# Encoder block on one core: where the raw weight tiles of the down projection are placed

## The chip, the cores and the metric

The kernel runs on one core of a Trainium2 chip. The metric is the device time of one execution in microseconds (us), the median of several runs; lower is better. A run is also profiled once: the hardware profiler records the start and the length of the engines' instructions and the transfers. The engines are PE (matmuls; PEld is its weight load), DVE (elementwise), ACT (activations and scaled copies), POOL (here a few elementwise operations and the issue of some transfers) and SP (which here only issues transfers).

## The reference, cut to what matters

One encoder layer over 512 tokens of width 2048 in float32: a combined input projection, two attention mixers, an output projection, and a gated feed-forward part. The change touches the last step of this:

```python
h2 = rmsnorm(x, g_ffn[layer])
gate, up = jnp.split(jnp.einsum('bsd,df->bsf', h2, w_gate_up[layer]), 2, axis=-1)
x = x + jnp.einsum('bsf,fd->bsd', jax.nn.silu(gate) * up, w_down[layer])
return rmsnorm(x, g_final)
```

`w_down` is 5632 x 2048, so the down projection multiplies 512 x 5632 by 5632 x 2048.

## The kernel before

**The product in seven.** A matrix product is done by 2 x 2 blocks with seven products instead of four times two (Winograd's form), called m1 to m7 in the code. Each takes one linear form of the activations (kept in the arena, a tile of 112 KB in each partition) and one of the weights. Weights arrive as raw tiles of 128 x 512 float32 (256 KB, 2 KB in each partition). For one pair of row blocks there are four of them, a, b, c and d. Where a form is a sum or a difference, DVE makes it in place (line 801, in `weights`).

**Three matmuls for one.** A float32 operand is split into a high part, which ACT copies (line 761, `split_hi`), and a low part, which DVE subtracts (line 764, `split_lo`). `mm3` (lines 235 to 237) multiplies high by high, high by low and low by high. The pair of parts stands in one of eight tiles called tw, taken in turn.

**Units.** A unit is one form of one pair: the two parts of its weights and six matmuls of 128 x 512. Units run in the order of a list. `ColBlock` makes the list of a column block: all pairs of m1, then m7 and m6, two units of m2, all of m5, the rest of m2, then m4 and m3. In the code's plan KEPT each raw tile is loaded once for a block and kept: a is last used by m5, b and d by m4, c by m3. When a form is done, ACT evicts two banks (line 1139, tile ev) and POOL adds them to memory by an accumulating transfer (line 1140); unit and bank orders make a few matmuls wait for that eviction.

**The down blocks.** `w_down` is done in six such blocks: three groups of row pairs (6, 8 and 8 pairs, `DOWN_PAIRS`) by two column halves. In this document they are blocks 0 to 5, with 42, 42, 56, 56, 56 and 56 units; units are counted from the first of block 0, so that block 1 begins at unit 42, block 2 at 84, block 3 at 140, block 4 at 196 and block 5 at 252. Raw tiles of these blocks are counted 1 to 176 in the order of their loads: 24 for a block of six pairs, 32 for one of eight. In a block, the a tiles come first, then c and b of each pair, then d.

**Reloaded forms.** The forms of the activations don't all fit in the arena. They lie in DRAM, and `next_forms` reloads a group of six or eight pairs during the block before: for each of the seven forms two loads, h = 0 (four pairs, 512 KB) and h = 1 (two or four pairs), issued from ACT's queue (line 1113), then split by ACT (line 1116) and DVE (line 1119) into the arena. The loads land in tiles called fr, two of 4 KB in each partition, taken in turn. This happens before block 0 (for six pairs), in blocks 1 and 2, and in blocks 3 and 4 (for eight pairs each).

**Who sets the order.** The program is written out in one order by hand (`manual_schedule`): for each unit `prepare` first loads what the planner allows, then makes weight parts for units up to 8 us ahead, then come the matmuls, then hooks (evictions, reloads). Loads are considered for units up to 20 us ahead (`load_raws`, line 1264 on). On each engine instructions run in this order, and only waits hold them: a load on SP may be issued long before its turn in the list if the place it goes to is free, and not before, and all later loads stand behind it. `live` holds the raw tiles whose last unit has not been prepared; `RAWS` limits their number, 21 for blocks of six pairs (tag draw6) and 28 for blocks of eight (draw8). Which place a new raw tile gets is not in the code: every load asks the pool for a new tile, and the builder gives it bytes that are free by then, among all tiles of the kernel.

**Memory and semaphores.** In the down blocks the arena, the eight tw tiles, six ev tiles, the fr tiles and two tiles of constants stand beside the raw tiles. The builder also counts the landings of the transfers of SP and ACT on eight semaphores in turn, in the order of the program.

Of the kernel before, what the change touches and what calls it, by code (L numbers as in the profile page):

```python
# [11 lines left out]
F32 = mybir.dt.float32  # L12
# [7 lines left out]
P = 128  # L20
# [27 lines left out]
PLAIN_WAIT = 5  # L48
SPILL_B = 6
TWINS = 8  # L50
RAWS = {"raw": 6, "craw": 24, "craw0": 24, "kraw": 9, "craw40": 18, "draw6": 21, "draw8": 28}
W_TILES = {"wi": 10, "wo": 12}
DOWN_PAIRS = (6, 8, 8)
ORDER = ("m1", "m7", "m6", "m2", "m4", "m5", "m3")
# [14 lines left out]
def encoder_block(ctx, tc, x, g_mix, w_in, g_q_a, g_k_a, g_out_a, g_out_b, w_out, g_ffn,  # L69
# [3 lines left out]
    wp = ctx.enter_context(tc.tile_pool(name="wstream"))  # L73
    dp = ctx.enter_context(tc.tile_pool(name="spill", bufs=1, space=bass.MemoryType.DRAM))
    sp = ctx.enter_context(tc.tile_pool(name="slots"))
# [5 lines left out]
    def nm(base):  # L81
        counter[0] += 1
        return f"{base}_{counter[0]}"
# [29 lines left out]
    homes = deque(stage[:, n] for n in range(20))  # L113
# [126 lines left out]
        return pair[0][:, lo:lo + n], pair[1][:, lo:lo + n]  # L240

    units = []
    twins, evs, frs = [], [], []

    def in_turn(tiles, n, shape, dtype, tag):
        if not tiles and homing[0]:
            whole = sp.tile([P, n] + shape[1:], dtype, tag=tag + "s", bufs=1, name=nm(tag))
            tiles.extend(whole[:, i] for i in range(n))
        if not tiles:
            tiles.extend(sp.tile(shape, dtype, tag=tag, bufs=n, name=nm(tag)) for _ in range(n))  # L250
        tiles.append(tiles.pop(0))
        return tiles[-1]

    class Raw:
# [3 lines left out]
        def load(self):  # L258
            if self.t is None:
                self.homed = bool(homes) and self.tag != "raw"  # L260
                self.t = homes.popleft() if self.homed else wp.tile([P, self.width], F32, tag=self.tag,
                                                                    bufs=RAWS[self.tag], name=nm("raw"))
                for src, dst in self.pieces(self.t):
                    nc.sync.dma_start(dst, src)
                if self.first:
                    load_x(self.first)
# [469 lines left out]
    def drain_until(cond):  # L736
        while not cond():
# [7 lines left out]
    KEPT = {"m1": (("a",), "a"), "m7": (("c", "b"), "b"), "m6": (("b", "a"), "b"), "m2": (("d",), "d"),  # L745
            "m5": (("c", "b"), "a"), "m4": (("d", "b"), "b"), "m3": (("c",), "c")}
# [356 lines left out]
    def next_forms(box, first, pairs):  # L1103
        seq = sorted(CHAIN, key=box.at.get)

        def ready(form, h):
            m, st = ORDER.index(form), {}
            lo_q, n = 4 * h, min(4, pairs - 4 * h)
            hi, lo = (form_tile(m, slice(lo_q, lo_q + n))[:, :, j] for j in range(2))

            def load():
                st["t"] = in_turn(frs, 2, [P, 4, 256], F32, "fr")[:, :n]
                nc.scalar.dma_start(st["t"], forms_dram[:, m, first + lo_q:first + lo_q + n])

            def split_hi():
                nc.scalar.activation(hi, st["t"], AF.Copy)  # L1116

            def split_lo():
                nc.vector.tensor_tensor(lo, st["t"], f32(hi), op=OP.subtract)  # L1119
            late = 4 * seq.index(form) + 4 * h  # L1120
            box.after(form, late - 5, load)
            box.after(form, late + 1, split_hi)
            box.after(form, late + 3, split_lo)
        for form in seq:
            for h in range(-(-pairs // 4)):
                ready(form, h)
# [1 line left out]
    gfin = {}  # L1128
    fin = {}
    def down_block(first, pairs, cb, last):  # L1130
        box = ColBlock(w_down, 2 * first * P, (cb * 1024, cb * 1024 + 512), pairs, KEPT, f"draw{pairs}",
                       close=finish if last else None)

        def add(form, i, j):
            def go():
                for t in range(2):
                    row = 2 * i + t
                    e = in_turn(evs, EVICT, [P, 512], F32, "ev")
                    nc.scalar.activation(e, box.bank_of(form)[t], AF.Copy, scale=r2["r"][:, row:row + 1])  # L1139
                    nc.gpsimd.dma_start(x1_dram[2 * cb + j, row], e, accum_op=OP.add)  # L1140
                if form in LAST_OF_BANK:
                    box.done(form)
            box.after(form, 0, go)

        def put(form, i, j):
            box.after(form, 0, lambda: [put_row(2 + j, 2 * i + t, box.bank_of(form)[t]) for t in range(2)])

        add("m1", 0, 0)
        add("m7", 1, 1)
        add("m6", 1, 0)  # L1150
        if last:
            done_rows = [(c, t) for c in range(2) for t in (2, 3, 0, 1)]
            for n in range(2):
                box.after("m7", 2 + 3 * n, lambda n=n: [load_gfin(n), load_x1(n, (2, 3)), load_x1(n, (0, 1))])
            box.after("m7", 7, lambda: [load_gfin(c) for c in (3, 2)])
            for n, (c, t) in enumerate(done_rows):
                box.after("m6", n - 2, lambda c=c, t=t: squares(c, t))
                box.after("m6", n, lambda c=c, t=t: gained(c, t))
            box.after("m6", 2, lambda: [load_x1(3, (2, 3)), load_x1(2, (0, 1)), load_x1(2, (2, 3)), load_x1(3, (0, 1))])
            put("m2", 0, 0)  # L1160
            put("m5", 1, 1)
            put("m4", 1, 0)
            for t in range(2):
                box.after("m4", -6 + t, lambda t=t: gained(2, t))
                box.after("m4", -4 + t, lambda t=t: gained(3, 2 + t))
            box.after("m4", 1, lambda: [row_scale(t) for t in (2, 3)])
        else:
            add("m2", 0, 0)
            add("m5", 1, 1)
            add("m4", 1, 0)  # L1170
            add("m3", 0, 1)
        return box
# [75 lines left out]
    def load_raws(n):  # L1248
        while done["load"] < len(units) and at[done["load"]] <= at[n] + units[done["load"]].load_ahead:
            for raw in units[done["load"]].raws:  # L1250
                if raw.t is None:
                    for r in live:
                        if last_use[r] < done["lo"] and r.homed and homing[0] and not any(r.t is h for h in retired):
                            homes.append(r.t)
                    live[:] = [r for r in live if last_use[r] >= done["lo"]]
                    if homing[0] and len(homes) <= (2 if xs[KD - 1] is None else 4 if done["load"] < 24 else 0):
                        return
                    if homing[0] and raw.tag == "raw" and sum(r.tag == "raw" for r in live) >= 2:
                        return
                    if sum((r.tag == "raw") == (raw.tag == "raw") for r in live) >= RAWS[raw.tag]:  # L1260
                        return
                    live.append(raw)
                    raw.load()
            done["load"] += 1
# [108 lines left out]
```

## Time and profile before

| | us |
|---|---|
| median of three runs | 2019.24 |
| lowest, highest | 2017.82, 2020.35 |
| the profiled execution: time | 2017.83 |
| the profiled execution: its span, first to last instruction | 2016.0 |

The mean granted clock of PE was 0.998. By the profile the first load of a down raw tile goes out at 1556 us, the last one at 1967 us.

How to read the rows shown below: times are us from the span's start unless marked ns. A row of the view by stages holds the stage, its length, then the busy time and the number of instructions of PE, PEld, DVE, ACT and POOL, the granted clock, the share of the 16 DMA engines that was busy, and GB/s. A row of the order of time holds the start, the length, the engine, the line of the code, the operation, what it writes and reads, how many were merged, and in brackets how long the engine had been idle and what ended that. "SPq" and "ACTq" are the issues of transfers. A row of waits holds who waited for what, the total, how often, and the longest. PE's matmuls overlap: the time from start to start is what counts. Some matmul records are missing.

### The profile page before, as it was taken

Reading aid. Unit: us, or ns where it says so; the run is one execution under the profiler, and the core shown is the slowest. Engines: PE = TensorE matmul, PEld = TensorE weight load, DVE = VectorE, ACT = ScalarE, POOL = GpSimd, SP = SyncE. Lnnn points to the kernel's source line nnn. Section 1 sums busy time; section 2 is a strip of 40 time slices with the busy share of each in tenths; the row PEclk is TensorE's granted clock in tenths of the full one; section 3 lists DMA queues with packets and bytes.
Section 4 is the critical chain, followed back from the end, with each engine's and each line's share of the span. In section 5 each row is a group of like instructions: output and inputs, shape, how many; then the busy total and the mean of one; then the engine's idle time right before and its main releaser. Section 6 shows DMA issues by size and latency. Waiting matters only on the chain. (4 is left out here: it accounts for less than half of the span.)

```text
span 2016.0 us, 27418 instructions
## 1 busy us (share of the span) xinstructions
PE 1987.8 (99%) x9019; PEld 1632.0 (81%) x9019; DVE 1573.0 (78%) x2781; ACT 1113.6 (55%) x1972; POOL 153.2 (8%) x172
## 2 busy tenths in 40 slices
PE   9999999999999999999999999999999999999998
PEld 6788887887788888888888888888888888788886
DVE  7988866576754688878877878778788987977967
ACT  7655345455543565555555555545545666666656
POOL 4200100000010000000000000000000121111121
PEclk9999999999999999999999999999999999999999
DMA  8576533335244545747647558458367699779865
GB/s 268 188 261 221 186 115 103 109 116 168 89 151 141 188 163 199 242 134 266 219 165 274 182 182 289 148 202 297 120 241 241 202 252 271 185 176 271 201 156 164
DMA packets 231391, 390.61 MB, mean 194 GB/s; under 512 B 21408, under 2 KB 70352, under 8 KB 231120
## 3 DMA queue, kind: packets, MB, share of 16 engines
q1 hardware_dynamic: 204880, 326.13, 48.3%
q0 software_dynamic: 14960, 33.04, 8.0%
q10 hardware_dynamic: 11408, 29.70, 4.2%
q8 instruction: 70, 1.15, 0.2%
q14 instruction: 73, 0.60, 0.1%
HBM read 325.08 MB, written 63.70 MB: 193 GB/s over the span
## 5 line engine op out<-in xcount | busy, mean ns | idle before, releaser
L235 PE MATMUL b<-tw,arena 128*128 128x512 f32 x2136 | 838.1, 392 | 2.2 <-ACT ev L1139 2.2
L237 PE MATMUL b<-tw,arena 128*128 128x512 f32 x2136 | 833.5, 390 | 2.8 <-DVE arena L332 2.6
L236 PE MATMUL b<-tw,arena 128*128 128x512 f32 x2136 | 833.2, 390 | 2.2 <-DVE tw L764 1.9
L761 ACT ACTIVATE tw<-raw 128x512 fp32r<-128x512 f32 x924 | 559.1, 628 | 440.4 <-DVE raw L801 284.8
L764 DVE TENSOR_TENSOR tw<-raw,tw 128x512 fp32r<-128x512 f32 x924 | 619.2, 687 | 170.8 <-ACT tw L761 167.5
L237 PEld LDWEIGHTS b<-tw,arena 128*128 128x128 f32 x2136 | 401.2, 188 | 89.9 <-DVE arena L332 6.1
L236 PEld LDWEIGHTS b<-tw,arena 128*128 128x128 f32 x2136 | 401.6, 188 | 88.0 <-DVE tw L764 5.9
L235 PEld LDWEIGHTS b<-tw,arena 128*128 128x128 f32 x2136 | 401.5, 188 | 84.3 <-ACT ev L1139 2.9
L801 DVE TENSOR_TENSOR raw<-raw,raw 128x512 f32<-128x512 f32 x528 | 361.5, 685 | 2.8 <-DMA raw<-in_w_gate_up_dram 2.6
L1140 POOL DMA_DIRECT2D x1d<-ev x76 | 66.4, 975 | 1150.7 <-ACT ev L1139 1138.6
L235 PE MATMUL b<-w,arena 128*128 128x512 f32 x368 | 146.1, 397 | 0.0
L237 PE MATMUL b<-w,arena 128*128 128x512 f32 x368 | 143.8, 391 | 0.0
L236 PE MATMUL b<-w,arena 128*128 128x512 f32 x368 | 143.4, 390 | 0.0
L237 PEld LDWEIGHTS b<-w,arena 128*128 128x128 f32 x368 | 69.1, 188 | 15.0
L236 PEld LDWEIGHTS b<-w,arena 128*128 128x128 f32 x368 | 69.2, 188 | 13.8
L235 PEld LDWEIGHTS b<-w,arena 128*128 128x128 f32 x368 | 69.1, 188 | 13.6
L761 ACT ACTIVATE tw<-stage 128x512 fp32r<-128x512 f32 x90 | 54.5, 628 | 42.2 <-DVE stage L801 33.8
L227 DVE TENSOR_TENSOR pTl<-b,pTh 128x512 fp32r<-128x512 f32 x64 | 44.0, 687 | 34.3 <-ACT pTh L226 24.0
L292 DVE TENSOR_TENSOR w<-raw,w 128x512 fp32r<-128x512 f32 x96 | 64.8, 684 | 6.0 <-ACT w L287 3.2
L355 DVE TENSOR_TENSOR pair<-pair 128x256 f32<-128x256 f32 x120 | 45.5, 421 | 26.5 <-ACT pair L996 25.5
L226 ACT ACTIVATE pTh<-b 128x512 fp32r<-128x512 f32 x64 | 38.0, 594 | 46.6 <-PE b L582 41.7
L1139 ACT ACTIVATE ev<-b,smalls 128x512 f32<-128x512 f32 x76 | 49.5, 682 | 25.4 <-PE b L237 25.3
(197 smaller groups left out, 1820.7 us busy)
## 6 DMA issues: line engine op xcount, KB each, us to landing
raw<-in_w_gate_up_dram SPq DMA_DIRECT2D x616, 256.0 KB, 5.3
raw<-in_w_down_dram SPq DMA_DIRECT2D x176, 256.0 KB, 6.9
stage<-in_w_in_dram SPq DMA_DIRECT2D x106, 256.0 KB, 4.6
forms<-pair SPq DMA_DIRECT2D x22, 896.0 KB, 5.3
x1d<-ev POOLq DMA_DIRECT2D x76, 256.0 KB, 6.6
fr<-forms ACTq DMA_DIRECT2D x35, 512.0 KB, 5.9
raw<-in_w_in_dram SPq DMA_DIRECT2D x64, 256.0 KB, 5.5
raw<-in_w_out_dram SPq DMA_DIRECT2D x32, 512.0 KB, 4.6
```

The source lines that it names most:

```text
L226: nc.scalar.activation(hi, src, AF.Copy)
L227: nc.vector.tensor_tensor(lo, src, f32(hi), op=OP.subtract)
L235: nc.tensor.matmul(dst, ah, bh, start=start, stop=False, skip_group_check=chained)
L236: nc.tensor.matmul(dst, ah, bl, start=False, stop=False, skip_group_check=chained)
L237: nc.tensor.matmul(dst, al, bh, start=False, stop=stop, skip_group_check=chained)
L292: nc.vector.tensor_tensor(self.w[1], self.src, f32(self.w[0]), op=OP.subtract)
L355: nc.vector.tensor_tensor(out, x, y, op=op)
L761: nc.scalar.activation(self.pair[:, 0], self.src, AF.Copy)
L764: nc.vector.tensor_tensor(self.pair[:, 1], self.src, f32(self.pair[:, 0]), op=OP.subtract)
L801: nc.vector.tensor_tensor(t[dst], t[src[0]], t[src[1]], op=OP.add if form == "m6" else OP.subtract)
L1139: nc.scalar.activation(e, box.bank_of(form)[t], AF.Copy, scale=r2["r"][:, row:row + 1])
L1140: nc.gpsimd.dma_start(x1_dram[2 * cb + j, row], e, accum_op=OP.add)
```

## The change

The raw tiles of blocks 0 to 4 come from a list of places (`pool`). A place is one tile of 2 KB, made by the kernel once and used again and again: when the last unit of a raw tile has been prepared, its place is put at the end of the list, and a load takes the place at the list's head, that is the one which has been free longest. A new place is made only when the list is empty, up to 21 in block 0 and up to 27 in blocks 1 to 4. For these blocks the limit on `live` no longer holds, only that on the places. Block 5 has a tag of its own ("last"), takes its tiles as before, and has the limit 28.

The fr tiles are no longer taken in turn from two of 4 KB. There is one for each pair of h and number of pairs: 4 KB for h = 0, 2 KB for h = 1 of the blocks of six pairs, 4 KB for h = 1 of those of eight.

```diff
-RAWS = {"raw": 6, "craw": 24, "craw0": 24, "kraw": 9, "craw40": 18, "draw6": 21, "draw8": 28}
+RAWS = {"raw": 6, "craw": 24, "craw0": 24, "kraw": 9, "craw40": 18, "draw6": 21, "draw": 27, "last": 28}
+POOLED = ("draw6", "draw")
...
-    twins, evs, frs = [], [], []
+    twins, evs, frs = [], [], {}
+    pool, made = deque(), [0]
...
-                self.t = homes.popleft() if self.homed else wp.tile([P, self.width], F32, tag=self.tag,
-                                                                    bufs=RAWS[self.tag], name=nm("raw"))
+                if self.tag in POOLED:
+                    if not pool:
+                        made[0] += 1
+                        pool.append(wp.tile([P, 512], F32, tag="pool", bufs=RAWS["draw"], name=nm("pool")))
+                    self.t = pool.popleft()
+                else:
+                    self.t = homes.popleft() if self.homed else wp.tile([P, self.width], F32, tag=self.tag,
+                                                                        bufs=RAWS[self.tag], name=nm("raw"))
...
-                st["t"] = in_turn(frs, 2, [P, 4, 256], F32, "fr")[:, :n]
+                if (h, n) not in frs:
+                    frs[h, n] = sp.tile([P, n, 256], F32, tag=f"fr{h}{n}", bufs=1, name=nm("fr"))
+                st["t"] = frs[h, n]
...
-        box = ColBlock(w_down, 2 * first * P, (cb * 1024, cb * 1024 + 512), pairs, KEPT, f"draw{pairs}",
+        box = ColBlock(w_down, 2 * first * P, (cb * 1024, cb * 1024 + 512), pairs, KEPT, "last" if last else "draw6" if first + cb == 0 else "draw",
                        close=finish if last else None)
...
+                        if last_use[r] < done["lo"] and r.tag in POOLED:
+                            pool.append(r.t)
...
-                    if sum((r.tag == "raw") == (raw.tag == "raw") for r in live) >= RAWS[raw.tag]:
+                    if raw.tag in POOLED:
+                        if not pool and made[0] >= RAWS[raw.tag]:
+                            return
+                    elif sum((r.tag == "raw") == (raw.tag == "raw") for r in live) >= RAWS[raw.tag]:
                         return
```

## The prediction

> **What bounds the kernel now.** I read the page first, then the stretch of the down blocks by stages, then PE's own order of time there, and then, going back from each stall, ACT, DVE and the queue of SP.
>
> ```profile
> span 2016.0 us, 27418 instructions
> PE 1987.8 (99%) x9019; PEld 1632.0 (81%) x9019; DVE 1573.0 (78%) x2781; ACT 1113.6 (55%) x1972; POOL 153.2 (8%) x172
> ...
> raw<-in_w_down_dram SPq DMA_DIRECT2D x176, 256.0 KB, 6.9
> ...
> fr<-forms ACTq DMA_DIRECT2D x35, 512.0 KB, 5.9
> ```
>
> PE works for 1987.8 of 2016.0 us, and the change gives it no work and takes none away. So it can win only where PE stands still in the down blocks (from about 1590 us), and lose only by making PE stand still there. The busy times of each engine in stages:
>
> ```profile
> 1600.00:1650.00 50.00, 49.44 (x223) 40.71 (x222) 40.19 (x66) 34.22 (x58) 12.22 (x14) 1.00 0.97 256
> 1650.00:1700.00 50.00, 50.00 (x222) 41.44 (x221) 39.13 (x57) 30.40 (x51) 8.69 (x10) 1.00 0.97 272
> 1700.00:1750.00 50.00, 46.89 (x201) 36.93 (x200) 45.55 (x68) 33.29 (x54) 8.67 (x10) 1.00 0.66 160
> 1750.00:1800.00 50.00, 50.00 (x222) 41.42 (x221) 37.14 (x60) 28.50 (x47) 6.99 (x8) 1.00 0.79 209
> ```
>
> The first number after the length is PE's: 3.11 us are missing in 1700 to 1750 (block 2), 0.56 us in 1600 to 1650, none beside. In an undisturbed stage 222 matmuls take 50 us, 0.225 us each, so a unit of six takes 1.36 us. The stalls one by one:
>
> ```profile
> 1705.74 0.39 PE L235 MATMUL b<-tw,arena 128*128 128x512 f32 x1
> 1706.65 0.50 PE L236 MATMUL b<-tw,arena 128*128 128x512 f32 x1 [0.52 <-DVE tw L764]
> 1706.99 0.40 PE L237 MATMUL b<-tw,arena 128*128 128x512 f32 x1
> ...
> 1712.00 0.39 PE L235 MATMUL b<-tw,arena 128*128 128x512 f32 x1
> 1712.61 0.50 PE L236 MATMUL b<-tw,arena 128*128 128x512 f32 x1 [0.22 <-DVE tw L764]
> ...
> 1717.95 0.39 PE L235 MATMUL b<-tw,arena 128*128 128x512 f32 x1
> 1718.93 0.50 PE L236 MATMUL b<-tw,arena 128*128 128x512 f32 x1 [0.59 <-DVE tw L764]
> ...
> 1734.20 0.40 PE L237 MATMUL b<-tw,arena 128*128 128x512 f32 x1
> 1736.26 0.50 PE L235 MATMUL b<-tw,arena 128*128 128x512 f32 x1 [1.66 <-ACT ev L1139]
> ```
>
> From start to start, less 0.23 us for the matmul itself, the four cost 0.68, 0.38, 0.75 and 1.83 us, together 3.64; the matmul after each starts 0.34 us on and not 0.23 (1706.65 to 1706.99), which makes 4.1 us in all. Every one waits for the low part of a weight pair (DVE, L764) or for an eviction that stands in ACT's queue behind the high parts. So DVE and ACT are late in block 2, and the reason lies 12 us earlier, on ACT and behind it DVE:
>
> ```profile
> 1683.07 1.14 ACT L761 ACTIVATE tw<-raw 128x512 fp32r<-128x512 f32 x2
> 1686.93 0.33 ACTq L1113 DMA_DIRECT2D fr<-forms  x1
> 1687.30 1.68 ACT L761 ACTIVATE tw<-raw 128x512 fp32r<-128x512 f32 x3 [3.10 <-DMA raw<-in_w_down_dram]
> 1688.88 1.24 ACT L1139 ACTIVATE ev<-b,smalls 128x512 f32<-128x512 f32 x2
> 1690.02 0.62 ACT L761 ACTIVATE tw<-raw 128x512 fp32r<-128x512 f32 x1
> 1694.39 0.33 ACTq L1113 DMA_DIRECT2D fr<-forms  x1
> 1694.77 1.16 ACT L761 ACTIVATE tw<-raw 128x512 fp32r<-128x512 f32 x2 [4.12 <-DMA raw<-in_w_down_dram]
> ```
>
> ```profile
> 1695.43 0.69 DVE L764 TENSOR_TENSOR tw<-raw,tw 128x512 fp32r<-128x512 f32 x1 [4.06 <-ACT tw L761]
> ```
>
> Twice ACT stands still until a raw tile has landed, and the first thing it then does is to issue a form load (L1113). The high part behind that (unit 84, the first of block 2) reads a tile loaded long before. The program counts the landings of SP's and ACT's transfers on eight semaphores taken in turn, and each transfer waits for the one eight places ahead of it in the program's order; the same wait stands on SP's own queue, where the waits are:
>
> ```profile
> SPq L264 <- DVE tw L764: 173.9, 63, 33.7
> SPq L264 <- DMA raw<-in_w_down_dram: 74.9, 70, 8.8
> ```
>
> (total, times, longest.) So a form load on ACT is late when raw tiles are late, and everything behind it on ACT is late with it. Why the raw tiles are late, in SP's order of time:
>
> ```profile
> 1635.14 27.45 SPq L264 DMA_DIRECT2D raw<-in_w_down_dram  x4
> ...
> 1661.59 34.30 SPq L264 DMA_DIRECT2D raw<-in_w_down_dram  x30
> ```
>
> ```profile
> SPq L264 <- DVE tw L764: 19.8, 1, 19.8
> ```
>
> In block 1 one load (the fourth of the six "d" tiles, number 46 of 176) keeps the queue shut for 19.8 us, since at most 21 raw tiles live at a time in the blocks of six pairs; number 46 gets the place of the first "a" tile of block 1, which unit 62 frees at 1661.6. Behind it stand loads whose places were free long before. Then 30 loads go out in 34.3 us, 1.14 us each, with the form loads between them:
>
> ```profile
> 1650.00:1655.00 5.00, 5.00 (x24) 4.14 (x23) 4.83 (x8) 2.44 (x5) 0.00 (x0) 1.00 0.63 98
> 1670.00:1675.00 5.00, 5.00 (x24) 4.14 (x23) 5.00 (x9) 2.51 (x5) 0.00 (x0) 1.00 1.08 310
> 1690.00:1695.00 5.00, 5.00 (x24) 4.14 (x23) 0.69 (x1) 0.88 (x3) 1.70 (x2) 1.00 1.06 382
> ```
>
> The last two columns are the DMA share and GB/s: 98 GB/s while the queue is shut, 310 and 382 afterwards, with all 16 engines full.
>
> **The change part by part.** *Block 1 may hold 27 tiles* (the second block's tag is now "draw"). By the code, loads 46 to 48 come when 21 places exist and none is free, so three are made, and all three loads go out behind number 45 at about 1637 us and on. Three transfers of 1.14 us, 3.4 us, leave the full stretch for the empty one. I take that as certain.
>
> *The places are taken in the order in which they came free.* I followed the list by hand. Load 49 now waits for unit 62, as number 46 did, 50 to 54 for units 63 to 67, and 55 for unit 72, though in the kernel before it waited for 65: with 24 places and not 27 in use, loads 55 to 72 lie about three units, 4 us, further back, and SP's queue rests from about 1669 to 1675. That is a loss of lookahead, but not yet of time: 72 is needed by unit 99, sixteen units (22 us) after its place comes free, against landing times of 6.9 us in the median.
>
> *What ACT then waits for.* Since three loads have gone ahead and those after lie three units back, fewer raw tiles stand before each form load in the order: the form load at 1686.93 waits for load 60 and no longer for 62, the one at 1694.39 for 65 and no longer for 68. Three loads of 1.14 us are 3.4 us, and the loads from 55 on start upon an empty DMA system instead of a full one, so their later start costs little. ACT's 4.12 us then shrink to 0.7. From below: nothing, if the loads lie further back by as much as they stand further ahead (4 us against 3.4). From above: all of 4.12. I take 3.4, nearest to the count of loads. The 3.10 us before it earn nothing of their own, because the evictions at 1688.88 wait for PE anyway. The gain goes through DVE, idle 4.06 us for that reason and without a pause in m7 and m6 of block 2, to PE: 3.4 of the 4.1 us lost there.
>
> *Two fixed form tiles* (4 KB a partition each, 2 KB for the second one of the blocks of six) take the place of a ring of two. The two halves of a form alternate in every reload, so each load follows the same last reader as before: no instruction, no wait, 0 us. It frees one place of 2 KB in block 0. What hides it is ACT's own order; without that, one wait for the split (L1119) of at most a few us in seven loads.
>
> *Blocks 0 and 3 to 5.* Loads 1 to 24 keep their order, 76 to 80 wait for units 110 to 114 as before (nine units ahead of need, 12 us), the last block keeps its 28. But the addresses of all tiles are dealt anew around 27 long-lived ones, and that cost stands in no row. Bounds: block 0 also shows such a wait (4.03 us of ACT before a form load), and 0.56 us of PE's idle time stand in that stage; so -0.6 us at best, and another stall like that of block 2, +4.1, at worst. I take 0, as the order of the loads is kept.
>
> ```profile
> 1578.35 0.33 ACTq L1113 DMA_DIRECT2D fr<-forms  x1
> 1578.78 1.15 ACT L761 ACTIVATE tw<-raw 128x512 fp32r<-128x512 f32 x2 [4.03 <-PE b L237]
> ```
>
> **The sum.** The profiled execution took 2017.83 us, 1.8 more than its span, and the median of three is 2019.24, 1.4 above it; I carry the difference over. 2017.83 - 3.4 = 2014.4, so 2019.24 - 3.4 = 2015.8, and as the small stalls of block 2 are not all in the 4.1, I say 2015.6.
>
> A rule against this: the Trainium skill, page "DMA: Bandwidth & Descriptors", section "Issuing engines are not separate DMA queues", says that transfers from all issuing engines end up on the same 16 DMA engines and that only the sequencer's issue time is saved by issuing elsewhere. By it, an order of loads creates no bandwidth, and where the share is 1.06 the gain would be nothing. The row of 1650 to 1655, with 0.63, shows that there is room to move loads into; the rival below is that rule at work.
>
> **The rivals.**
>
> *Bandwidth decides.* Loads 55 to 75 begin at 1675 instead of 1669, 21 loads at 1.14 us are 24 us, and they end at 1699 where they ended at 1696 before; form loads share the engines with them, so ACT waits as it did. For it: shares above 1 from 1670 to 1695. Against it: what ACT waits for stands three loads further ahead. Gain 0 to 1: 2019.
>
> *More than the stall.* With SP never shut in block 1 and ACT's waits gone in blocks 0 and 2, all idle time of these stages goes: 4.1 + 0.6 us and the rest of the slow starts, about 6: 2013. For it: the waits have one cause. Against it: nothing in the list changes loads 1 to 24.
>
> *The list hands out later in block 3 (slower).* The reload before block 4 is of the same kind. There load 116 waits for unit 180 and no longer for 178, and 117 to 121 for 181 to 185, two to four units later than before; four units are 5.4 us. If the raw tiles then land 5.4 us later, the form load at the start of block 4 holds ACT as 1694.39 did, PE loses 4.1 us there, and if block 2's stall stays too: 2019.24 + 4.1 = 2023.3. It decides once a raw tile that a form load waits for lands more than about 4 us later than now, for then the lead of DVE is used up:
>
> ```profile
> 1848.14 0.33 ACTq L1113 DMA_DIRECT2D fr<-forms  x1
> 1848.57 2.20 ACT L761 ACTIVATE tw<-raw 128x512 fp32r<-128x512 f32 x4 [1.71 <-PE b L237]
> ```
>
> Here ACT's pause before that load ends on PE and is 1.71 us: it is ahead, and the loads have room. For it: the order by hand. Against it: the pause.
>
> *The change doesn't do what it says:* the order of places before was nearly first in, first out already (the places of 76 to 80 are the same). That falls under the first rival.
>
> **How the numbers follow.** A measurement of this kernel tells about 0.2% (4 us) from no change, so faster means under 2015.2. Forecast 2015.6, own range 2013.5 to 2017: 0.43, a little over half of it under 2015.2 (0.24 faster, 0.19 the same). More than the stall: 0.20, faster. Bandwidth decides: 0.12, the same. Slower in block 3 or by the new addresses: 0.25. Faster 0.44, same 0.31, slower 0.25. The range leaves out about a tenth on either side: 2012.0 below, 2023.5 above.
>
> **What would show it.** Right: four loads or more behind each other at 1636 to 1641, ACT's pauses before the form loads at 1687 and 1694 under 1 us, PE without a stall in 1700 to 1750. Wrong: those pauses still 3 to 4 us (bandwidth), a new pause before a form load near 1848 with PE idle after 1855 (the list hands out later), SP shut in front of one of the first 24 loads (addresses), or a difference outside the down blocks.

## The result, and the profile after

The changed kernel takes 2021.82 us in the median of 19 runs (2020.81 to 2023.86), the kernel before 2018.79 us (19 runs beside them). The ratio is 1.0017, 95% interval 1.0011 to 1.0023: slower by 3.4 us, where 3.6 us were forecast to be won. The profiled execution took 2021.63 us, 3.80 more than that of before. The page, and the down blocks by stages (the columns as before):

```profile
span 2019.5 us, 27428 instructions
PE 1988.7 (98%) x9019; PEld 1631.7 (81%) x9019; DVE 1573.5 (78%) x2781; ACT 1114.1 (55%) x1972; POOL 153.7 (8%) x172
```

```profile
1600.00:1650.00 50.00, 50.00 (x225) 41.22 (x224) 39.52 (x64) 32.48 (x57) 10.73 (x13) 1.00 0.97 262
1650.00:1700.00 50.00, 47.47 (x206) 38.73 (x205) 37.27 (x56) 29.82 (x50) 8.74 (x10) 0.99 0.93 246
1700.00:1750.00 50.00, 47.78 (x202) 38.13 (x202) 45.40 (x68) 32.55 (x53) 7.16 (x9) 0.98 0.67 168
1850.00:1900.00 50.00, 49.18 (x215) 39.67 (x214) 42.64 (x64) 29.88 (x48) 7.00 (x8) 1.00 0.75 190
```

The work is the same. PE is busy for all of 1600 to 1650, where 0.56 us were missing before; 2.53 and 2.22 us are missing around the start of block 2, and 0.82 us in block 4, where nothing was missing before.

Both traces hold the same 9019 matmuls in the same order, so the start of each can be subtracted from the start of its twin, and the growth of that difference tells where time went: blocks 0 and 1 -0.97 us (of which -0.71 at the stall of 1609), block 2 +3.25, block 4 +1.77, all the rest -0.25; together 3.80. The expectations below speak of block 2's loss as 3.2 us and of block 0's win as 0.97.

The stalls of block 2 begin where ACT stands still. Its order of time in the changed kernel, at the same place as before:

```profile
1685.75 0.33 ACTq L1123 DMA_DIRECT2D fr<-forms  x1
1686.12 1.68 ACT L769 ACTIVATE tw<-pool 128x512 fp32r<-128x512 f32 x3 [2.68 <-DMA pool<-in_w_down_dram]
...
1688.85 0.62 ACT L769 ACTIVATE tw<-pool 128x512 fp32r<-128x512 f32 x1
1696.32 0.33 ACTq L1123 DMA_DIRECT2D fr<-forms  x1
1696.69 1.15 ACT L769 ACTIVATE tw<-pool 128x512 fp32r<-128x512 f32 x2 [7.22 <-DMA pool<-in_w_down_dram]
```

The pause that the forecast let shrink from 4.12 to 0.7 us is 7.22 us long. PE has then used up its lead (PE's order of time):

```profile
1694.68 0.39 PE L238 MATMUL b<-tw,arena 128*128 128x512 f32 x1
1697.37 0.50 PE L236 MATMUL b<-tw,arena 128*128 128x512 f32 x1 [2.31 <-ACT tw L769]
...
1699.29 0.63 PE L238 MATMUL b<-tw,arena 128*128 128x512 f32 x1
1699.72 0.63 PE L236 MATMUL b<-tw,arena 128*128 128x512 f32 x1
...
1738.18 0.50 PE L236 MATMUL b<-tw,arena 128*128 128x512 f32 x1 [1.67 <-ACT ev L1149]
...
1892.24 0.50 PE L236 MATMUL b<-tw,arena 128*128 128x512 f32 x1 [0.76 <-ACT ev L1149]
```

Two matmuls start 2.69 us apart (1694.68 to 1697.37), and a little later eight follow each other at 0.43 us in place of 0.23; the last section comes back to them. In block 4 ACT shows the same picture, where the forecast's slower rival had looked for it (before: 1.71 us before the load at 1848.14):

```profile
1849.95 2.20 ACT L769 ACTIVATE tw<-pool 128x512 fp32r<-128x512 f32 x4 [2.14 <-DMA pool<-in_w_down_dram]
1857.42 0.33 ACTq L1123 DMA_DIRECT2D fr<-forms  x1
1857.85 0.63 ACT L769 ACTIVATE tw<-pool 128x512 fp32r<-128x512 f32 x1 [5.71 <-DMA pool<-in_w_down_dram]
```

And SP. Loads 46 to 48 do go out at 1639, as forecast; then the queue is shut for 16.1 us until unit 62, and again until 1674.54, when unit 72 hands its place to load 55 (SP's order of time; SP's waits from 1640 to 1662 and from 1668 to 1675):

```profile
1639.18 1.70 SPq L272 DMA_DIRECT2D pool<-in_w_down_dram  x3
...
1674.54 1.65 SPq L272 DMA_DIRECT2D pool<-in_w_down_dram  x2
```

```profile
SPq L272 <- DVE tw L772: 16.1, 1, 16.1
...
SPq L272 <- DVE tw L772: 6.2, 2, 5.7
```

What this leaves of the DMA engines, in two stages of 5 us, the kernel before first (last columns: DMA share, GB/s):

```profile
1675.00:1680.00 5.00, 5.00 (x24) 4.14 (x23) 4.29 (x7) 2.95 (x6) 1.76 (x2) 1.00 1.06 371
1680.00:1685.00 5.00, 5.00 (x24) 4.14 (x23) 3.58 (x6) 4.21 (x7) 1.72 (x2) 1.00 1.08 307
```

```profile
1675.00:1680.00 5.00, 5.00 (x24) 4.14 (x23) 4.80 (x8) 2.95 (x6) 1.17 (x2) 1.00 0.80 152
1680.00:1685.00 5.00, 5.00 (x24) 4.14 (x23) 3.58 (x6) 3.44 (x6) 1.75 (x2) 1.00 0.98 291
```

In these 10 us the changed kernel moves 2.2 MB and the kernel before 3.4 (GB/s times 5 us, summed). That is 1.2 MB, between four and five raw tiles, and three of them had been moved ahead. When the places come at last the engines are full again, and not with raw tiles alone. The queues from 1685 to 1695 (packets, MB, share of 16 engines; q1 is SP's queue, q0 POOL's with the additions of results, L1150), the kernel before first, then the changed one:

```profile
q1 hardware_dynamic: 1189, 2.16, 59.0%
q0 software_dynamic: 352, 0.66, 35.5%
```

```profile
q1 hardware_dynamic: 982, 1.78, 50.1%
q0 software_dynamic: 449, 0.83, 45.0%
```

Raw load 65, for which the second form load waits, and 68, for which it waited before (the last number is the time from issue to landing, us; changed kernel, then before):

```profile
pool<-in_w_down_dram SPq DMA_DIRECT2D x1, 256.0 KB, 11.1
```

```profile
raw<-in_w_down_dram SPq DMA_DIRECT2D x1, 256.0 KB, 9.2
```

Load 65 goes out at 1685.10 and lands at 1696.22; load 68 of the kernel before went out at 1685.13 and landed at 1694.30. That the form load now waits for an earlier load bought nothing.

### The profile page after: what moved, and what is told of

It reads as the page before. It is cut to its first block, busy times and chain, and to the rows that moved or that the text cites. A ratio compares the mean times of both kernels' runs of the same rounds, so it can differ in the third digit from the quotient of the medians.

```text
span 2019.5 us, 27428 instructions
## 1 busy us (share of the span) xinstructions
PE 1988.7 (98%) x9019; PEld 1631.7 (81%) x9019; DVE 1573.5 (78%) x2781; ACT 1114.1 (55%) x1972; POOL 153.7 (8%) x172
## 5 line engine op out<-in xcount | busy, mean ns | idle before, releaser
L769 ACT ACTIVATE tw<-raw 128x512 fp32r<-128x512 f32 x672 | 408.9, 629 | 333.4 <-DVE raw L809 211.6
L772 DVE TENSOR_TENSOR tw<-raw,tw 128x512 fp32r<-128x512 f32 x672 | 450.5, 687 | 111.8 <-ACT tw L769 110.2
L809 DVE TENSOR_TENSOR raw<-raw,raw 128x512 f32<-128x512 f32 x384 | 263.0, 685 | 1.1 <-DMA raw<-in_w_gate_up_dram 1.1
L772 DVE TENSOR_TENSOR tw<-pool,tw 128x512 fp32r<-128x512 f32 x252 | 169.0, 688 | 65.3 <-ACT tw L769 64.6
L769 ACT ACTIVATE tw<-pool 128x512 fp32r<-128x512 f32 x252 | 150.6, 627 | 112.2 <-DVE pool L809 75.0
L1150 POOL DMA_DIRECT2D x1d<-ev x76 | 66.5, 982 | 1153.5 <-ACT ev L1149 1141.1
L809 DVE TENSOR_TENSOR pool<-pool,pool 128x512 f32<-128x512 f32 x144 | 98.7, 685 | 0.0
```

The costliest lines, as they stand in the source:

```text
L769: nc.scalar.activation(self.pair[:, 0], self.src, AF.Copy)
L772: nc.vector.tensor_tensor(self.pair[:, 1], self.src, f32(self.pair[:, 0]), op=OP.subtract)
L809: nc.vector.tensor_tensor(t[dst], t[src[0]], t[src[1]], op=OP.add if form == "m6" else OP.subtract)
```

## The experiments

Each was timed in five rounds against the kernel before. "Pause" is ACT's before the second form load of block 2; the blocks are differences of matmul starts against the kernel before, in the one profiled execution, in us, block 2 from its first unit on; "slow" is the part of block 2 in matmuls 0.43 us apart.

| run | ratio to before (95%) | pause | block 2 (slow) | block 4 |
|---|---|---|---|---|
| kernel before | 1 | 4.12 | 0 (0) | 0 |
| changed kernel | 1.0017 (1.0011 to 1.0023) | 7.22 | +3.25 (1.56) | +1.77 |
| block1_27 | 1.0007 (0.9998 to 1.0015) | 6.08 | +3.03 (1.57) | 0.00 |
| freed_order | 0.9995 (0.9987 to 1.0004) | 6.44 | +2.65 (1.63) | 0.00 |
| early_places | 1.0028 (1.0018 to 1.0038) | 7.51 | +2.87 (1.59) | +1.36 |
| early_freed | 1.0004 (0.9995 to 1.0013) | 5.33 | +0.42 (0) | 0.00 |
| forms_only | 0.9992 (0.9983 to 1.0001) | 3.35 | -0.35 (1.20) | 0.00 |
| list_only | 1.0020 (1.0011 to 1.0029) | 7.17 | +2.81 (0) | +1.45 |
| half_loads | 0.9987 (0.9978 to 0.9996) | 2.60 | -0.92 (1.20) | +1.75 |
| plain_writes | 0.9996 (0.9987 to 1.0005) | 3.97 | -1.33 (0) | +1.61 |
| forms_on_sp | 0.9981 (0.9972 to 0.9989) | none | -3.58 (0) | 0.00 |
| sp_list_order | 0.9984 (0.9975 to 0.9993) | none | -3.47 (0) | 0.00 |
| sp_early_freed | 0.9980 (0.9971 to 0.9989) | none | -3.30 (0) | 0.00 |
| sp_forms_only | 0.9976 (0.9966 to 0.9986) | none | -3.76 (0) | 0.00 |

The ratio is of medians, and the profiled execution isn't the median one: among others, those of freed_order and half_loads are the slowest of their eleven (2.5 and 2.0 us above the median), those of early_freed and early_places the fastest of theirs (1.5 us below). So the ratios say which kernel is faster, and the last columns where the time went in one execution.

Block 2 less its slow part follows the pause roughly, with one of ten kernels out of line (list_only, +2.81 at 7.17): 2.60 gives -2.12, 3.35 gives -1.55, 4.12 gives 0, 5.33 gives +0.42, 6.44 gives +1.02, 7.22 gives +1.69.

**block1_27: the forecast's gain by itself.**

```diff
-RAWS = {..., "draw6": 21, "draw8": 28}
+RAWS = {..., "draw6": 21, "draw": 27, "draw8": 28}
...
-        box = ColBlock(..., KEPT, f"draw{pairs}",
+        box = ColBlock(..., KEPT, "draw" if (first, cb) == (0, 1) else f"draw{pairs}",
```

> The kernel before with one edit: the second block of six pairs may hold 27 raw tiles instead of 21; the builder still deals the places, and the form tiles stay as they were. By the addresses of the built program loads 46 to 48 then wait for units 35 to 37 (before: 62, 35, 36), and from 49 on every load waits for the same unit as before; the form loads at the start of block 2 still stand eight places behind raw loads 62 and 68. Theory (lookahead: the changed kernel lost because its loads 55 to 72 wait for later units): with those units unchanged and three loads moved ahead, load 68 goes out 2 to 4 us earlier than 1685.1, the pause of ACT of 4.12 us before its form load at 1694 shrinks to 0.5 to 2.5, and of the 4.05 us that PE loses in block 2 only 0 to 2 are left: ratio to the kernel before 0.9982 to 0.9992. Rival (bandwidth): the tiles land when they did, the ratio is 0.9997 to 1.0003.

The theory falls. With every later load waiting for the unit it waited for before, three loads moved ahead still win nothing. Load 68 goes out 1.3 us sooner than before (1683.87), where 2 to 4 were expected, but takes 12.1 us to land, and the pause grows (landing of load 68, and ACT's order of time):

```profile
raw<-in_w_down_dram SPq DMA_DIRECT2D x1, 256.0 KB, 12.1
```

```profile
1696.03 0.33 ACTq L1113 DMA_DIRECT2D fr<-forms  x1
1696.41 1.15 ACT L761 ACTIVATE tw<-raw 128x512 fp32r<-128x512 f32 x2 [6.08 <-DMA raw<-in_w_down_dram]
```

The loads that count, 58 to 75, wait for units 70 to 83 in both kernels, so they cannot use engines left free before that. The interval holds no change, as the bandwidth rival had it.

The loads moved ahead have a price of their own. ACT now waits for a raw tile before it issues the form load at 1643.72 in block 1; the kernel before has no such wait there (ACT's order of time):

```profile
1644.15 1.15 ACT L761 ACTIVATE tw<-raw 128x512 fp32r<-128x512 f32 x2 [4.42 <-DMA raw<-in_w_down_dram]
```

PE then loses 0.96 us at 1665, still in block 1, at an eviction. In the changed kernel this pause is 2.41 us and costs nothing, in early_places 4.34 us and 0.58 us of PE.

**freed_order: the list sorted by who reads last.**

```diff
-                    for r in live:
+                    for r in sorted(live, key=lambda r: last_use[r] - 2 * (r is not units[last_use[r]].raws[-1])):
```

> The changed kernel with one edit: places that come free in the same look are put on the list by the unit that last reads them (a tile whose last reader is the sum of a pair counts as two units earlier than the sum's destination), not in the order in which they were loaded. By the addresses loads 84 to 99 and 116 to 131 then wait for the units of the kernel before (84: 122 and not 124, 89: 125 and not 129, 116: 178 and not 180, 121: 181 and not 185), and 55 for unit 70 and not 72; the lag of three loads in block 1 (24 places) stays. Theory (order within the list costs block 4, lag and order together cost block 2): matmul by matmul against the kernel before, the 1.77 us lost in block 4 are gone (under 0.3), the 3.23 us lost in block 2 shrink to 0 to 2, and the 0.97 us won in block 0 stay: ratio 0.9995 to 1.0006. Rival (bandwidth decides in block 2, addresses in block 4): both losses stay, 1.0013 to 1.0020.

As the theory said, with a ratio on its lower edge: block 4 loses nothing and its stage is full (first row), while the pause in block 2 is only 0.8 us shorter (second).

```profile
1850.00:1900.00 50.00, 50.00 (x223) 41.40 (x222) 44.90 (x68) 32.98 (x53) 7.00 (x8) 1.00 0.74 191
```

```profile
1695.19 1.15 ACT L769 ACTIVATE tw<-pool 128x512 fp32r<-128x512 f32 x2 [6.44 <-DMA pool<-in_w_down_dram]
```

Its block 2 lost 2.65 us in the profile, above the 0 to 2 expected; 1.63 of these are slow matmuls, which are not in every execution, and this execution was its slowest. By the medians the order is worth all that the change lost, 1.0017 to 0.9995. The list appends places that come free in the same look in the order of their loading. When the planner looks again after a rest, places that come free two to four units later stand in front, and SP, which issues in order, waits for them.

**early_places and early_freed: 27 places in use sooner**, without and with that order.

```diff
-                    if not pool:
+                    made[1] += 1
+                    if not pool or made[1] >= 43 and made[0] < RAWS[self.tag]:
                         made[0] += 1
-                        pool.append(...)
+                        pool.appendleft(...)
```

> The changed kernel with one edit: from down load 43 on a new place is made ahead of the list as long as fewer than 27 exist, so 27 places are in use from load 48 on, and not from load 75 on. By the addresses loads 49 to 51 wait for units 39 to 41 (changed kernel: 62 to 64), 55 for 65 (72), 65 for 73 (77); the order within the list stays, so 84 and 116 still wait for 124 and 180. Theory (lag of three loads is the larger part of block 2's loss): block 2 loses 0 to 3 us less than the kernel before lost there, so 3.2 to 6 us less than the changed kernel; block 4 keeps its 1.77 us. Ratio to the kernel before 0.9990 to 1.0005. Rival (bandwidth): 1.0013 to 1.0020 as the changed kernel.

> Both edits of the two runs beside it: 27 places in use from load 48 on, and the list in the order of the last reader. From load 49 on every load then waits for the same unit as in the kernel before (within one), and 46 to 48 for units 22 to 26. Theory: no loss in block 4, block 2 as with the 27 tiles of block 1 alone (0 to 2 us left of 4.05), the 0.97 us of block 0 kept: the fastest of the four, ratio 0.9977 to 0.9990, which would show that the idea was sound and the two orders spoilt it. Rival (bandwidth): 0.9992 to 0.9998, by block 0 alone.

Both theories fall. More places sooner did not help: early_places is no faster than the changed kernel (7.51 us of pause, block 2 nearly as bad), and early_freed, whose waits are the best of the four, is at no change, where 0.9977 to 0.9990 was expected. The four kernels with the list can be read as two by two: the order of the last reader takes 1.0017 to 0.9995 and 1.0028 to 1.0004, about 0.23% each time; 27 places sooner take 1.0017 to 1.0028 and 0.9995 to 1.0004, about 0.1% the wrong way, within what the intervals leave open. So the loss comes from the order in the list and not from the lag of three places. block1_27 and early_freed have nearly the same waits and differ by 2.6 us in block 2, 1.6 of it slow matmuls; their medians differ by 1 us, and the rest stays open.

**forms_only and list_only: the two parts of the change alone.** Diffs: the change's hunks on the form tiles alone, and all others.

> The kernel before with the two fixed form tiles alone; raw tiles dealt by the builder under the old limits. In the changed kernel 0.97 us were won in block 0 (the stalls at 1566 and 1609 of the kernel before are not there); the run with block 1 at 27 tiles kept the one at 1608, the three runs with the list lost it. Theory A (as predicted: the form tiles are worth nothing, the win is the list's): the stall near 1609 stays, ratio 0.9997 to 1.0004. Theory B (the win is the form tiles': the second tile of a block of six is 2 KB instead of 4): no stall near 1609, ratio 0.9992 to 0.9998. For block 2 load 46 waits for unit 62 as before, so both say its loss stays at about 4 us.

> The changed kernel with the old ring of two form tiles: the list alone. By the addresses every load from 49 on waits for the unit it waits for in the changed kernel. Theory (the loss is the list's): block 2 and block 4 lose against the kernel before as in the changed kernel (3.2 and 1.8 us), ratio 1.0013 to 1.0025; by theory A of the run beside it the 0.97 us of block 0 are won here too, by theory B not. Rival (list and form tiles lose together only): 0.9997 to 1.0005.

The loss is the list's, 1.0020. The form tiles win in the trace: between 1590 and 1650 forms_only gains 0.69 us and list_only 0.00; the ratio of forms_only, 0.9992, lies on the edge of theory B, and its interval just holds no change. Its block 2, which both theories left as it was, is 0.35 us shorter in spite of 1.20 us of slow matmuls; no run shows why. With the ring, the first of two evictions stands on ACT until PE has done transposes; with fixed tiles it stands ahead of that wait, and only the second one waits (ACT's order of time, list_only first, then the changed kernel):

```profile
1608.64 0.69 ACT L1147 ACTIVATE ev<-b,smalls 128x512 f32<-128x512 f32 x1 [1.22 <-PE b L1076]
```

```profile
1606.68 0.68 ACT L1149 ACTIVATE ev<-b,smalls 128x512 f32<-128x512 f32 x1
1607.68 0.69 ACT L1149 ACTIVATE ev<-b,smalls 128x512 f32<-128x512 f32 x1 [0.33 <-PE b L1076]
```

Theory B of the expectation is right about whose the win is. What the trace shows of the reason is where one wait of ACT stands; whether the size of a tile brought that about, as theory B had it, or the tiles' being fixed, is not shown.

**half_loads and plain_writes: less work for the DMA engines, with the changed kernel's waits.**

```diff
+                r.thin = row == 12 * P and lo[0] == 0
...
+                    fresh = not pool
...
+                    if self.tag in POOLED and self.thin and not fresh:
+                        src, dst = src[:, :256], dst[:, :256]
                     nc.sync.dma_start(dst, src)
```

```diff
-                    nc.gpsimd.dma_start(x1_dram[2 * cb + j, row], e, accum_op=OP.add)
+                    nc.gpsimd.dma_start(x1_dram[2 * cb + j, row], e,
+                        **({} if first == 6 and cb == 0 or (first, cb) == (0, 1) else dict(accum_op=OP.add)))
```

> The changed kernel in which 29 of the 32 raw loads of block 2 (all but the three that fill new places) bring only the first 256 of 512 columns; the right half of those tiles keeps old weights. Order, waits and number of transfers stay. It takes 29 x 0.57 = 16.5 us of DMA work out of block 2. Theory (bandwidth: from about 1675 to 1700 all engines are full, and raw load 65, for which the form load of ACT waits, lands when the bytes ahead of it are through, 11.1 us after its issue): it lands within 6 us of its issue and is issued earlier as well, the 7.22 us pause of ACT shrinks under 2.5, PE stands still in block 2 for under 1 us, and against the changed kernel 3.5 to 5 us are won: ratio to the kernel before 0.9993 to 1.0003. Rival (late issue: places come free too late, whatever the bandwidth): the pause stays over 4 us and PE loses 2 us or more in block 2, ratio 1.0005 to 1.0015.

> The changed kernel in which the results of blocks 1 and 2 are written over the residual rows, and not added to them (the accumulation of these two blocks is left out). Waits, order and number of transfers stay; from 1685 to 1695 the adding transfers took 45% of the engines' time for 0.83 MB, raw tiles 50% for 1.78 MB, so twice as much time for a byte. Theory (bandwidth, shared with the adding transfers): written plainly they take half, the raw loads get about a fifth more, load 65 lands 1.5 to 3 us sooner after its issue than 11.1 us, ACT's pause of 7.2 us becomes 4 to 6, block 2 wins 1.5 to 3.5 us against the changed kernel: ratio to the kernel before 1.0000 to 1.0010. Rival (the adding transfers do not matter): pause over 6.5 us, 1.0013 to 1.0021.

The first diff leaves out half the columns of 29 raw tiles of block 2, the second writes the results of blocks 1 and 2 without adding. ACT's order of time in half_loads, then in plain_writes:

```profile
1691.21 1.15 ACT L772 ACTIVATE tw<-pool 128x512 fp32r<-128x512 f32 x2 [2.60 <-DMA pool<-in_w_down_dram]
```

```profile
1692.25 1.15 ACT L769 ACTIVATE tw<-pool 128x512 fp32r<-128x512 f32 x2 [3.97 <-DMA pool<-in_w_down_dram]
```

Both confirm bandwidth, with the changed kernel's waits for places, and both win more than expected, 6 and 4 us against the changed kernel. The pauses lie just outside what was expected (under 2.5, and 4 to 6). In half_loads two signs were missed: raw load 65 lands 7.2 us after its issue and not within 6, and PE stands still for 1.72 us in 1700 to 1750 and not under 1, nearly all of it 1.68 us before 1732.90, at an eviction that no run with form loads on ACT got rid of. In plain_writes raw load 65 lands 8.3 us after its issue and not 11.1, and the queues from 1685 to 1695 read

```profile
pool<-in_w_down_dram SPq DMA_DIRECT2D x1, 256.0 KB, 8.3
```

```profile
q1 hardware_dynamic: 1358, 2.48, 64.5%
q0 software_dynamic: 320, 1.05, 26.0%
```

A quarter of the engines' time for 1.05 MB written plainly, against 45% for 0.83 MB added: 25 against 54 points for a MB. Block 4 keeps its 1.6 to 1.8 us in both, since neither touched its loads.

**forms_on_sp and its variants: nothing on ACT to wait.**

```diff
-                nc.scalar.dma_start(st["t"], forms_dram[:, m, first + lo_q:first + lo_q + n])
+                nc.sync.dma_start(st["t"], forms_dram[:, m, first + lo_q:first + lo_q + n])
```

> The changed kernel with the list in the order of the last reader (the run freed_order), and the form loads issued by SP instead of ACT; the scheduler of the build places them anew among the raw loads (in block 2 behind raw loads 58, 66 and 72, eight places behind 52, 59 and 66). Theory (late raw tiles become PE's time only through ACT, which stands before the form load): ACT has no pause before unit 84 of more than 1 us, DVE keeps its lead, PE stands still in block 2 for under 1 us where freed_order lost some 3.9 and the kernel before 4.05: ratio 0.9972 to 0.9985. Rival (the split of the form then waits for its landing on ACT, and SP, held by the form loads, issues raw tiles later): the stall moves to the split, ratio 0.9992 to 1.0010.

> The changed kernel, list order unchanged (load 55 waits for unit 72, 116 for 180), with the form loads issued by SP. Theory (late raw tiles reach PE only through ACT standing before a form load): the order of the list then no longer matters, PE stands still for under 1 us in block 2 and under 0.5 us in block 4, ratio 0.9975 to 0.9990, within 0.1% of forms_on_sp (0.9981). Rival (the order costs by itself, the raw tiles come too late for the high parts): 1.5 us or more are lost in block 4, ratio 0.9990 to 1.0010.

> forms_on_sp with the places made early as well (27 in use from load 48 on; loads 49 to 51 wait for units 39 to 41 and not 62 to 64). Theory (PE has no stall of block 2 left to win): no difference to forms_on_sp, ratio to the kernel before 0.9977 to 0.9987. Rival (more places still win, up to the 0.5 us left in block 2 and more in block 5): under 0.9977.

> The kernel before with the two fixed form tiles and the form loads issued by SP, without the list: raw tiles dealt by the builder, at most 21 in block 1. Load 46 still keeps SP shut until unit 62, at about 1661, and two form loads of block 1 now stand behind it in SP's order. Theory (the place of issue does it, the list is not needed): block 2 loses under 1 us, ratio 0.9976 to 0.9986. Rival (a shut SP holds the form loads, the list is needed for the move): PE stands still in block 1 or 2 for 2 us or more, ratio 0.9990 to 1.0020.

All four beat both kernels, with 3.3 to 3.8 us won in block 2. Of the stalls of block 2 one is left, 0.8 to 1.2 us at the eviction near 1732, in sp_list_order a little more than the 1 us expected. In forms_on_sp ACT now pauses only for PE in this stretch (its order of time; then SP's, and two stages):

```profile
1687.75 1.66 ACT L769 ACTIVATE tw<-pool 128x512 fp32r<-128x512 f32 x3
1689.31 1.05 ACT L1126 ACTIVATE arena<-fr 128x1024 fp32r<-128x1024 f32 x1
1690.26 1.66 ACT L769 ACTIVATE tw<-pool 128x512 fp32r<-128x512 f32 x3
1694.64 1.37 ACT L1149 ACTIVATE ev<-b,smalls 128x512 f32<-128x512 f32 x2 [2.72 <-PE b L238]
```

```profile
1678.16 0.33 SPq L1123 DMA_DIRECT2D fr<-forms  x1
...
1684.51 0.33 SPq L1123 DMA_DIRECT2D fr<-forms  x1
```

```profile
1650.00:1700.00 50.00, 50.00 (x222) 41.41 (x221) 41.19 (x61) 34.04 (x55) 10.43 (x12) 1.00 0.94 247
1700.00:1750.00 50.00, 49.05 (x217) 40.30 (x216) 46.93 (x72) 31.80 (x51) 6.93 (x8) 1.00 0.80 201
```

sp_list_order has the list's own order and shows no stall in block 4 either. In forms_on_sp raw load 65 goes out at 1689.68 and lands at 1699.81, 3.6 us later than in the changed kernel, and PE doesn't stand still there: in these runs a late raw tile costs PE time only where a form load on ACT waits for it. sp_early_freed is level with forms_on_sp, as its theory said. sp_forms_only, without any list and with SP still shut by load 46, is as good as the others (0.9976; the intervals overlap): the list is not needed, and its rival fell. One thing these runs don't separate: on SP the form loads also go out sooner (1678 and 1684 in place of 1686 and 1696), as the build places them ahead of more raw loads.

The Trainium skill, page "DMA: Bandwidth & Descriptors", section "Issuing engines are not separate DMA queues", which the prediction cites, lets one expect nothing of this move but some issue time. That holds for bandwidth (0.94 of the engines' time in 1650 to 1700, as in the changed kernel's 0.93). What the move wins is the wait: on ACT high parts whose raw tiles had long landed stood behind it, for 4.12 us in the kernel before and 7.22 us in the changed one.

## Why the prediction was wrong, point by point

*Block 1 may hold 27 tiles; loads 46 to 48 go out at 1637 and on.* Right: 1639.18, three in a row. But that they "leave the full stretch for the empty one", taken as certain, is not what happened. They landed at 1648.5 to 1651, in a stretch that was nearly full already; the one with room, from 1650, was left as empty as before (0.66 against 0.63), since SP was shut again (two stages of the changed kernel; the first had 0.88 and 197 before):

```profile
1645.00:1650.00 5.00, 5.00 (x23) 4.13 (x23) 4.67 (x8) 4.34 (x8) 1.76 (x2) 1.00 1.00 322
1650.00:1655.00 5.00, 5.00 (x23) 4.13 (x22) 4.90 (x8) 2.37 (x5) 0.00 (x0) 1.00 0.66 102
```

*The order followed by hand, 55 waiting for unit 72, SP resting until 1675.* Right: 1674.54.

*"That is a loss of lookahead, but not yet of time", and "What ACT then waits for".* This is the step that failed. It named the right loads (the second form load now waits for load 65 and no longer for 68) and the right delay of their issue (65 goes out 3.55 us later than before, 4.9 against PE, which was 1.3 us ahead by then; 4 had been worked out), and then said that they "start upon an empty DMA system instead of a full one, so their later start costs little". The empty system was wasted, at 152 GB/s from 1675 to 1680, since no load had had a place until 1674.54; and when the places came, all loads came together with the additions of results. Load 65 landed after 11.1 us, not sooner than the 9.6 of before. The pause became 7.22 in place of 0.7 us; the term of -3.4 us was +3.25, of which 1.56 us are the slow matmuls of that execution. Two things stand behind this. The lookahead lost to the list's order did cost time: freed_order, which takes that order away, is level with the kernel before (0.9995). And block1_27 shows that the 3.4 us are not won even without the lag: three loads went out sooner, and those behind them waited as before.

*Two fixed form tiles, 0 us.* Wrong by 0.7 us in the trace, shown by forms_only against list_only. The reasoning looked at waits of the form tiles and not at what a build does with the order around them.

*Blocks 3 to 5, 0 us.* Wrong. The slower rival, the list handing out later in block 3, is what happened. Load 121 in SP's order of time, the kernel before first, then the changed one:

```profile
1828.62 0.33 SPq L264 DMA_DIRECT2D raw<-in_w_down_dram  x1
```

```profile
1836.03 0.33 SPq L272 DMA_DIRECT2D pool<-in_w_down_dram  x1
```

That is 7.4 us later, 5.5 against PE, which was 1.9 us late by then; 5.4 had been worked out for its four units. The form load at 1857.42 holds ACT for 5.71 us, and PE loses 1.77 us, where the rival's price was 4.1; that the lead of DVE took more of it is likely and not shown. freed_order shows the cause: the order within one look.

*The bandwidth rival* had the mechanism of block 2 right, and its times: loads 55 to 75 were to begin at 1675 and end at 1699, and went out from 1674.54 to 1698.90. Its price was wrong: it allowed 0 to 1 us of gain and no loss. The sum by measured terms: -0.97 + 3.25 + 1.77 - 0.25 = 3.80, against a forecast of -3.6.

## What to carry to other kernels

Count a load as moved ahead only if there is room where it goes and if the transfers behind it may start sooner as well: if these wait for places, an engine freed earlier is an engine idle earlier. (The second half is a reading of block1_27; no run let the later loads start much sooner.) A list that takes the longest-free place is only as good as its order, so put places on it by their last reader and not by their loading. And a transfer that may have to wait doesn't belong on an engine that feeds the critical path: moving it to SP was worth 0.2% against the kernel before, with which the best of the lists is level.

## What the runs showed of the hardware

A stall of PE can cost twice. After the 2.31 us of idle time at 1697 eight matmuls started 0.43 us apart and not 0.23 (rows above: 1699.29 to 1699.72), 1.56 us more, with the granted clock at 0.89 and then 0.77 in the stages of 5 us from 1695 and 1700. Six or eight such matmuls, 1.2 to 1.6 us, stand in six of the profiled executions, each time within about 2 us of a stall; a stall of 1.87 us in list_only and one of 1.68 us in plain_writes had none after them. So two executions with nearly the same stalls can differ by 1.6 us in block 2. The Trainium skill, page "TensorE: Matmul & The Clock Gate", section "Part 1: The HAM clock gate (the "warmup" mystery)", describes this state, half the clock until a window of about 3.4 us has been busy; the eight matmuls, 3.4 us in all, agree. It names an idle window of that length as the condition; here 1.7 to 2.3 us of idle time were enough at times.

Adding transfers from POOL take twice the engines' time of plain ones (54 against 25 points for a MB, above), and two or three of them at a time took nearly as much as the seven or so raw loads in flight, 45.0% against 50.1%. The Trainium skill, page "DMA: Bandwidth & Descriptors", section "Queues, rings and completion order", says that each engine goes round the queues that have work for it, packet by packet. These rows don't test that: POOL's queue moved 449 packets and SP's 982, of nearly the same size (1.8 KB), and no run shows whether POOL's queue had work at every turn.
